# Around the turn from attention to MLP: squares summed earlier, three output-projection tiles ahead of the MLP's buffers, fewer small transfers, two loads issued from GpSimd

## The chip, the core and the metric

The kernel runs on one core of one Trainium2 chip. Its engines are TensorE (PE, matmuls; PEld is its weight load), VectorE (DVE), ScalarE (ACT), GpSimd (POOL) and SyncE (SP), which here does nothing but issue DMAs, in order. The metric is the device time of one execution in microseconds (us); lower is better.

## The reference

One step of a hybrid decoder layer in fp32: 512 prompt columns and 8 samples of 8 new columns (NT = 576 columns in all), model width D = 2048.

```python
h = x + W_out [ FoX(RMSNorm(x)) || DSA(RMSNorm(x)) ]
y = h + ConvGatedMLP(RMSNorm(h))
...
def rms_norm(x, g):
    y = xf * lax.rsqrt(jnp.mean(xf * xf, axis=-1, keepdims=True) + EPS)
    return y * g
...
def conv_ffn(hn, prev_g, w_gate, w_up, conv_w, conv_b, w_down):
    g = hn @ w_gate
    u = hn @ w_up
    gp = jnp.concatenate([prev_g, g], axis=1)
    gc = conv_b + sum(conv_w[j] * gp[:, j:j + T] for j in range(CONV_W))
    return (silu(gc) * u) @ w_down, gp[:, T:]
```

FoX is an attention with forget gates (8 heads), DSA a sparse attention over keys picked by an indexer (8 heads). The samples also attend to 1024 cached positions. The MLP's hidden width is 5504, which is 43 tiles of 128; its gate branch goes through a convolution of width 3 over positions, whose earlier rows come from the input `state_ffn_conv`, and whose last rows are outputs.

## The kernel before

Everything lies transposed in memory: 128 rows of the model dimension on the partitions, columns of the batch along the free axis. The 576 columns are cut in two halves of 288 (HALF): the first half is prompt alone, the second is the other 224 prompt columns and the 64 sample columns. A product of fp32 accuracy is made of three matmuls: each weight tile is cast to its upper part (ACT, `upper`, L1572 for the MLP's pools, tile `wu`), the rest is the lower part (DVE, `lower`, L1577, `wl`), and the matmuls are upper by upper, upper by lower and lower by upper (L1584, L1585, L1587).

Stages, in the order of the span: the input projection and the prompt's attention; the sample's DSA; the sample's FoX attention (`fox_scores`, `fox_values`), during which the output projection's other products fill TensorE (`w_out_a`, `w_out_late`, L171 to L173 with tile `rawT`, stored to the buffer `hdr` in DRAM); then the turn to the MLP; 43 items of gate and up projection; the down projection.

The turn is what the change rebuilds. It begins when the last sample's FoX result (`osum`) is turned and split into `gxs`. Three things follow in the code:

- The pools of the attention are closed and those of the MLP opened on the same memory. `wload` (L1566) brings a weight tile of 512 KB into one of four buffers `wr`.
- The loop over the 16 output tiles (`for o in range(KD)`): each tile's second half lacks the FoX heads' part, 8 products of 3 matmuls. The sum is added to `h` in DVE (L1667) and stored (L1668). `square` (L1592 to L1596) squares the tile's second half and two tiles of the first half on ACT and adds them up on DVE in `ssum`.
- `norm` makes the inverse root of the mean square from `ssum` by a matmul with ones (L1607) and Newton steps on DVE, and spreads it along the partitions as `rb`. `half0` normalizes the first half (16 multiplications `normed_h`, L1628) and splits it into `xh`, `xl` (L196 on ACT, L199 on DVE); it is a generator that the loop steps once per tile from the ninth tile on. `half1` does the same for the second half, interleaved with the first half's products (`products(0)` to `products(7)`), which are stored in the DRAM buffer `pdr`.

In the items, `states(j)` loads the convolution's earlier rows, eight DMAs of 16x128 for eight items (L1697); `last_rows(j)` collects seven items' last rows and stores them with fourteen DMAs (L1718, L1719). For the first eight items (`pre`), the products in `pdr` come back into `p1` and `gx` (L1907, L1908).

The order on each engine is not written out: a scheduler places the instructions of the whole program by its own estimate of times; where a tile's buffer is freed by an earlier user, the new user waits by semaphore. SP issues its DMAs strictly one after the other, so one that waits holds up all behind it.

## Time and profile before

| | us |
|---|---|
| median of three runs (2961.52, 2961.62, 2963.15) | 2961.62 |
| profiled execution | 2966.47 |
| its span | 2964.4 |
| PE busy in the span | 2773.7 (94%) |
| DVE busy | 2135.4 (72%) |
| ACT busy | 1414.1 (48%) |
| POOL busy | 501.6 (17%) |

Times in rows are counted from the start of the span. TensorE is the engine with the most work, and its busy time is close to the span, so what can be gained on it is idle time and time at the lower granted clock (PEclk, a share of full speed; about 0.5 is the lower level). In 700 us of the items, from 1650 to 2350, it is never idle. Matmuls are pipelined: the distance between two starts is what one costs, not the duration in its row. A bracket at a row's end is the engine's idle time before it and what ended that.

### The profile page before, as it was taken

The numbers are of one execution on the slowest core, as the hardware profiler recorded it, in microseconds if no ns is written. First come the engines' busy times: TensorE is split into PE (matmuls) and PEld (weight loads), VectorE is DVE, ScalarE is ACT, GpSimd is POOL, SyncE is SP. The second block draws the span as 40 slices with busy tenths as digits, with TensorE's granted clock in tenths as the row PEclk, the third lists the DMA queues.
The fourth block names the chain that finished last, engine by engine and source line by source line (L and its number), as shares of the span: only waits on it lengthen the run. The fifth ranks groups of instructions, "written<-read, shape, count | busy, mean of one in ns | idle before, by whom it ended". The sixth has DMA issues, their size and how long they took to land.

```text
span 2964.4 us, 52612 instructions
## 1 busy us (share of the span) xinstructions
PE 2773.7 (94%) x19863; PEld 2653.4 (90%) x19863; DVE 2135.4 (72%) x3732; ACT 1414.1 (48%) x2458; POOL 501.6 (17%) x579
## 2 busy tenths in 40 slices
PE   2999999999998999988989999999999989898998
PEld 2899899999898888868889999999999989888898
DVE  2667769656646656657977777777777789898996
ACT  2445753665755556654533444444444433333332
POOL 0223233423554133330000000000000000000000
PEclk7999999999999999989999999999999989999999
DMA  3523343335747788867544343343343353333333
GB/s 78 150 59 102 97 115 96 104 98 145 194 126 222 229 280 285 274 200 224 167 126 136 108 116 105 101 122 106 100 119 108 99 188 110 110 106 96 106 97 111
DMA packets 530956, 408.61 MB, mean 138 GB/s; under 512 B 41668, under 2 KB 472902, under 8 KB 530190
## 3 DMA queue, kind: packets, MB, share of 16 engines
q1 hardware_dynamic: 527294, 394.50, 45.4%
q0 software_dynamic: 3408, 10.75, 1.2%
q8 instruction: 156, 2.56, 0.4%
q14 instruction: 98, 0.80, 0.1%
HBM read 354.95 MB, written 49.95 MB: 137 GB/s over the span
## 4 chain that ended last, share of the span: by engine, by line
PE 50%; DVE 9%; DMA 7%; issue 2%; ACT 1%; SPq 1%; POOL 0%; DVEq 0%; ACTq 0%; POOLq 0%
PE pgemm L1584 8%; PE pgemm L1585 8%; PE pgemm L1587 7%; PE pone L1584 6%; PE pone L1585 5%; PE pone L1587 5%; DVE wl L1577 3%; DMA wr<-in_w_up_dram 2%; PE pone L1394 2%; DMA wr<-in_w_down_dram 1%; DVE ht L2084 1%; PE pgemm L171 1%; PE pgemm L172 1%; PE pgemm L173 1%; PE pout L1464 1%
## 5 line engine op out<-in xcount | busy, mean ns | idle before, releaser
L172 PE MATMUL pgemm<-xl,wh 128*128 128x288 f32 (+1 forms) x1696 | 512.2, 302 | 52.4 <-DVE xl L305 52.4
L171 PE MATMUL pgemm<-xh,wh 128*128 128x288 f32 (+1 forms) x1824 | 551.1, 304 | 4.7 <-DVE rawT L1340 2.1
L173 PE MATMUL pgemm<-xh,wl 128*128 128x288 f32 (+1 forms) x1824 | 550.4, 302 | 0.7 <-DVE wl L152 0.7
L172 PEld LDWEIGHTS pgemm<-xl,wh 128*128 128x128 f32 (+1 forms) x1696 | 322.3, 190 | 59.2 <-DVE xl L305 53.6
L171 PEld LDWEIGHTS pgemm<-xh,wh 128*128 128x128 f32 (+1 forms) x1824 | 346.0, 190 | 13.9 <-DVE rawT L1340 2.4
L1572 ACT CAST wu<-wr 128x1024 fp32r<-128x1024 f32 (+1 forms) x229 | 223.1, 978 | 275.0 <-PE pgemm L1585 109.3
L173 PEld LDWEIGHTS pgemm<-xh,wl 128*128 128x128 f32 (+1 forms) x1824 | 346.4, 190 | 6.6 <-issue 1.2
L1584 PE MATMUL pgemm<-xh,wu 128*128 128x288 f32 x1104 | 309.1, 303 | 39.4 <-DVE ht L2084 24.0
L1577 DVE TENSOR_TENSOR wl<-wr,wu 128x1024 fp32r<-128x1024 f32 (+1 forms) x229 | 258.3, 1133 | 120.9 <-ACT wu L1572 116.5
L1572 ACT CAST wu<-x 128x1024 fp32r<-128x1024 f32 x172 | 180.6, 1050 | 268.1 <-DVE x L1848 156.9
L1584 PEld LDWEIGHTS pgemm<-xh,wu 128*128 128x128 f32 x1104 | 212.8, 193 | 45.0 <-issue 20.4
L1584 PE MATMUL pgemm<-hi,wu 128*128 128x288 f32 x784 | 218.2, 303 | 5.4 <-DVE ht L2084 2.7
L1709 POOL COPY cn<-gx 128x2 f32<-128x2 f32 x43 | 45.8, 1065 | 1013.5 <-DVE gx L1725 1013.5
L1577 DVE TENSOR_TENSOR wl<-x,wu 128x1024 fp32r<-128x1024 f32 x172 | 209.1, 1219 | 1.6 <-ACT wu L1572 0.5
L1585 PE MATMUL pgemm<-lo,wu 128*128 128x288 f32 x760 | 209.9, 300 | 0.0
L1585 PE MATMUL pone<-xl,wu 128*128 128x288 f32 x768 | 208.9, 297 | 0.0
L1572 ACT CAST wu<-sum 128x768 fp32r<-128x768 f32 (+1 forms) x112 | 95.2, 850 | 234.7 <-DVE sum L1848 114.3
L1585 PE MATMUL pgemm<-xl,wu 128*128 128x288 f32 x680 | 185.8, 298 | 0.0
L1587 PE MATMUL pgemm<-xh,wl 128*128 128x288 f32 x1104 | 181.1, 297 | 0.0
L152 POOL TENSOR_TENSOR wl<-wraw,wh 128x1024 fp32r<-128x1024 f32 (+1 forms) x51 | 122.0, 2392 | 338.9 <-ACT wh L151 336.9
L151 ACT CAST wh<-wraw 128x1024 fp32r<-128x1024 f32 (+1 forms) x122 | 127.1, 1042 | 97.5 <-PE pgemm L172 89.9
L1584 PE MATMUL pone<-hi,wu 128*128 128x288 f32 x536 | 150.9, 304 | 19.9 <-ACT wu L1572 15.8
(616 smaller groups left out, 7377.1 us busy)
## 6 DMA issues: line engine op xcount, KB each, us to landing
wr<-in_w_gate_dram SPq DMA_DIRECT2D x102, 512.0 KB
wraw<-in_w_in_dram SPq DMA_DIRECT2D x88, 512.0 KB
wr<-in_w_up_dram SPq DMA_DIRECT2D x86, 512.0 KB
wr<-in_w_down_dram SPq DMA_DIRECT2D x112, 384.0 KB
kraw<-in_cache_fox_k_dram SPq DMA_DIRECT2D x128, 256.0 KB
vraw<-in_cache_fox_v_dram SPq DMA_DIRECT2D x128, 256.0 KB
wraw<-in_w_out_dram SPq DMA_DIRECT2D x32, 512.0 KB
dkraw<-in_cache_dsa_k_dram SPq DMA_DIRECT2D x64, 128.0 KB
```

The lines of the kernel that those rows point to most:

```text
L151: A.copy(h[:, :k, :m], raw[:, :k, :m])
L152: (G if share[0] and not u else V).tensor_sub(l[:, :k, :m], raw[:, :k, :m], f(h)[:, :k, :m])
L171: T.matmul(acc[:m, :], h[:, j, :m], xh[:, c], start=kt == 0, stop=False)
L172: T.matmul(acc[:m, :], h[:, j, :m], xl[:, c], start=False, stop=False)
L173: T.matmul(acc[:m, :], l[:, j, :m], xh[:, c], start=False, stop=kt == nk - 1)
L1394: T.transpose(pp[:, g * P:(g + 1) * P], raws[h // 4 * 4 + g][:, h % 4 * P:(h % 4 + 1) * P], ident)
L1572: A.copy(h[:, :n], t[:, :n])
L1577: V.tensor_sub(l[:, :n], t[:, :n], f(h)[:, :n])
L1584: T.matmul(acc, wh, xh, start=start and k == 0, stop=False, skip_group_check=not start)
L1585: T.matmul(acc, wh, xl, start=False, stop=False, skip_group_check=not start)
L1587: T.matmul(acc, wl, xh, start=False, stop=k == len(rows) - 1, skip_group_check=not start)
L1709: G.tensor_copy(c[:, j % CN, 0:2], gx[:, TP:TP + 2])
```

## The change

The first half's columns are complete in `w_out_a` and `w_out_late`, so their squares are taken there (`square0`), ACT and DVE each once per tile, and the inverse root `yn0` is made at the attention's end (`inverse_rms`), before the MLP's pools open. Three (NW) of the sixteen second-half tiles are computed at that place too, with weights that `load_w` has fetched into the attention's own buffers, and are stored to `hdr`; the loop in the MLP's pools then has thirteen tiles, and `half0` steps from the fifth tile on. Its sums alternate between two kinds of PSUM buffers. A group of eight loads of earlier rows becomes one DMA, a group of fourteen stores of last rows two. The loads from `pdr` are issued by GpSimd instead of SP.

```diff
+NW = 3
...
-    jobs += [([w_out[:1024, o * P:(o + 1) * P]], 8, P) for o in range(NLATE)]
+    jobs += [([w_out[:1024, o * P:(o + 1) * P]], 8, P) for o in (*range(NLATE), *range(NW))]
...
                 V.tensor_add(d, acc, d)
+                if o >= NLATE and not hh:
+                    square0(d)
...
             V.tensor_add(hx, acc, hx)
+            square0(hx)
...
+    def square0(d):
+        if not begun:
+            begun.append(1)
+            A.activation(ssum0, d, AF.Square)
+            return
+        sq = sx.tile([P, HALF], F32, name="sq0", bufs=2)
+        A.activation(sq, d, AF.Square)
+        V.tensor_add(ssum0, ssum0, sq)
...
+    yn0 = const.tile([P, 3], F32, name="yn0")
+    inverse_rms(sx, yn0, [ssum0])
+    for o in range(NW):
+        hx = wp.tile([P, NT], F32, name="rawT", bufs=3)[:, :HALF]
+        S.dma_start(hx, hdr[o, :, HALF:])
+        units = ready.pop(0)
+        prefetch(1)
+        gemm(units, gxs, P, lambda _, acc: V.tensor_add(hx, acc, hx), (1,))
+        S.dma_start(hdr[o, :, HALF:], hx)
     sx_ctx.close()
     sk_ctx.close()
...
     def half0():
-        yield from norm(ssum[0])
+        along(yn0)
+        yield
...
-    for o in range(KD):
-        load_wo(o + 4)
...
+    for o in range(NW, KD):
+        load_wo(o - NW + 4)
...
-        acc = psum_g()
+        acc = psum_g() if o % 2 else psum_s()[:, :HALF]
...
-        sq1 = square(o, 1)
-        if o < 8:
-            square(2 * o, 0)
-            square(2 * o + 1, 0)
-        else:
-            next(fox0, None)
+        if o - NW < NW:
+            square(o - NW)
+        sq1 = square(o)
         if o == 3:
             taps()
+        if o > 3:
+            next(fox0, None)
...
-            for i in range(m):
-                S.dma_start(st[i * 16:(i + 1) * 16, :], state[:, (j + i) * P:(j + i + 1) * P])
+            S.dma_start(st[:m * 16, :], state[:, j * P:(j + m) * P].rearrange("r (i c) -> i r c", c=P))
...
+            S.dma_start(cvp[:, jj].rearrange("r (i c) -> i r c", c=P), co[:m * 2, :])
+            S.dma_start(cvs[:, jj].rearrange("r (i c) -> i r c", c=P), co[m * 2:m * 18, :])
...
-            S.dma_start(p1, pdr[j, 0])
-            S.dma_start(gx[:, 2:2 + HALF], pdr[j, 1])
+            G.dma_start(p1, pdr[j, 0])
+            G.dma_start(gx[:, 2:2 + HALF], pdr[j, 1])
```

How the order moves at three places follows; line numbers of the changed kernel are one to some forty higher.

On SP, at the turn, before: after the convolution's taps (`gx`) come a load of `h` and at once the weights of the loop.

```order
L1554 DMA gx<-in_conv_w_dram 43x128 x3
L1555 DMA gx<-in_conv_b_dram 43x128
L1539 DMA x_17378<-hdr 128x4x288
L1566 DMA wr<-in_w_out_dram 128x8x128 x3
L1539 DMA x_17380<-hdr 128x8x288
L1539 DMA x_17379<-hdr 128x8x288
L1566 DMA wr<-in_w_out_dram 128x8x128
L1697 DMA stt<-in_state_ffn_conv_dram 16x128 x7
L1566 DMA wr<-in_w_out_dram 128x8x128
```

And in the changed kernel:

```order
L1596 DMA gx<-in_conv_w_dram 43x128 x3
L1597 DMA gx<-in_conv_b_dram 43x128
L1731 DMA stt<-in_state_ffn_conv_dram 128x1x128
L1551 DMA hdr<-rawT 128x288 x3
L1731 DMA stt<-in_state_ffn_conv_dram 128x1x128
L1608 DMA wr<-in_w_out_dram 128x8x128 x2
L1581 DMA x_17558<-hdr 128x2x288
L1608 DMA wr<-in_w_out_dram 128x8x128
L1581 DMA x_17558<-hdr 128x2x288
L1581 DMA x_17560<-hdr 128x8x288
```

The stores of the three tiles, each of which needs its tile's sum, now stand ahead of the first weight load of the loop, and so does the second load of earlier rows; the row of seven small loads is gone.

On DVE, at the end of the loop, before: the 16 multiplications of `half0`, the splits `xh` and `xl`, and then the first operation of the second half's norm (`ms`).

```order
L1596 TENSOR_TENSOR ssum_17390<-ssum_17390,sq 128x288
L1628 SCALAR_TENSOR_TENSOR x_17380<-x_17380,g_144,rb 128x288 x8
L1628 SCALAR_TENSOR_TENSOR x_17379<-x_17379,g_144,rb 128x288 x8
L1667 TENSOR_TENSOR x_17381<-pgemm,x_17381 128x288
L1577 TENSOR_TENSOR wl<-wr,wu 128x1024
L199 TENSOR_TENSOR xh<-x_17380,xh 128x8x288
L199 TENSOR_TENSOR xl<-x_17379,xl 128x8x288
L1611 TENSOR_SCALAR ms<-pone 128x2
```

In the changed kernel the same multiplications stand behind the third and fourth weight tile of the loop:

```order
L1619 TENSOR_TENSOR wl<-wr,wu 128x1024 x3
L1703 TENSOR_TENSOR x_17558<-pgemm,x_17558 128x288
L1703 TENSOR_TENSOR x_17558<-pone,x_17558 128x288
L1655 SCALAR_TENSOR_TENSOR x_17560<-x_17560,g_144,rb 128x288 x8
L1655 SCALAR_TENSOR_TENSOR x_17559<-x_17559,g_144,rb 128x288 x8
L1638 TENSOR_TENSOR ssum<-ssum,sq 128x288
L1703 TENSOR_TENSOR x_17558<-pgemm,x_17558 128x288
L1619 TENSOR_TENSOR wl<-wr,wu 128x1024
L200 TENSOR_TENSOR xh<-x_17560,xh 128x8x288
```

They have moved from the loop's end to its beginning, and with them the splits.

On PE, at the last sample of the attention, before: behind the transposes of the probabilities (L785, L790) come 31 filler matmuls of the output projection up to the first product with the values (`pout`), and 8 more behind the sixth; the last of these rows and what follows:

```order
L171 MATMUL pgemm<-xh,wh 128x288
L1464 MATMUL pout<-svh,ptile 64x512
L1465 MATMUL pout<-svl,ptile 64x512
L1464 MATMUL pout<-svh,ptile 64x512
L1465 MATMUL pout<-svl,ptile 64x512
L1464 MATMUL pout<-svh,ptile 64x512
L1465 MATMUL pout<-svl,ptile 64x512
L172 MATMUL pgemm<-xh,wh 128x288
```

In the changed kernel:

```order
L786 MATMUL pone<-ident,bt 128x64 x8
L791 MATMUL pone<-ident,bt 8x64
L173 MATMUL pgemm<-xh,wh 128x288
L174 MATMUL pgemm<-xh,wl 128x288
L172 MATMUL pgemm<-xh,wh 128x288
L173 MATMUL pgemm<-xh,wh 128x288
L174 MATMUL pgemm<-xh,wl 128x288
L172 MATMUL pgemm<-xh,wh 128x288
L173 MATMUL pgemm<-xh,wh 128x288
L174 MATMUL pgemm<-xh,wl 128x288
L1479 MATMUL pone<-ident,ob 128x64 x4
L1468 MATMUL pout<-svh,ptile 64x512
```

Eight filler matmuls stand there and none behind the sixth product; the other 31 are done before the transposes. Behind the last product come the sums of squares (L1510) and the 72 matmuls of the three tiles.

## Rows read from the trace of the kernel before

**Rows 1.** Stretches of the span: start and end us, length, then busy time of PE, PEld, DVE, ACT and POOL (number of instructions), the granted TensorE clock, the DMA engines' busy share and GB/s.

```profile
1280.00:1300.00 20.00, 20.00 (x124) 15.99 (x123) 9.90 (x19) 11.60 (x19) 8.64 (x6) 1.00 0.58 179
...
1320.00:1340.00 20.00, 13.33 (x85) 13.20 (x86) 7.75 (x15) 7.70 (x13) 0.00 (x0) 0.74 0.93 261
...
1360.00:1380.00 20.00, 19.37 (x146) 18.94 (x146) 16.63 (x40) 11.69 (x20) 0.00 (x0) 1.00 1.09 312
1380.00:1400.00 20.00, 13.26 (x78) 12.34 (x77) 19.34 (x43) 7.92 (x8) 0.00 (x0) 0.77 0.44 129
...
1460.00:1620.00 160.00, 142.03 (x1000) 139.92 (x999) 122.84 (x172) 59.82 (x66) 4.67 (x16) 0.95 0.47 136
1650.00:2350.00 700.00, 700.00 (x5276) 699.78 (x5275) 523.75 (x662) 321.97 (x417) 42.71 (x62) 1.00 0.38 108
```

**Rows 2.** The chain of waits from 1318 to 1330 us: start, us, what.

```profile
1320.65 5.59 DMA wr<-in_w_out_dram
1326.26 1.05 ACT wu L1572
```

**Rows 3.** PE instructions in time order, from the last sample's first `pout` to the fourth tile of the loop: start us, duration us, line, operation, output and inputs, shapes, count, and the idle time before with its releaser.

```profile
1303.39 0.40 PE L1464 MATMUL pout<-svh,ptile 128*64 128x512 f32 x1
...
1319.45 0.39 PE L1465 MATMUL pout<-vn,ptile 8*64 8x512 f32 x1
...
1327.36 0.61 PE L1584 MATMUL pgemm<-xh,wu 128*128 128x288 f32 x1 [6.16 <-ACT wu L1572]
...
1328.96 0.44 PE L1584 MATMUL pgemm<-xh,wu 128*128 128x288 f32 x1
1329.20 0.44 PE L1585 MATMUL pgemm<-xl,wu 128*128 128x288 f32 x1
...
1338.29 1.22 PE L1587 MATMUL pgemm<-xh,wl 128*128 128x288 f32 x8
...
1345.07 0.29 PE L1585 MATMUL pgemm<-xl,wu 128*128 128x288 f32 x1
1345.20 0.29 PE L1584 MATMUL pgemm<-xh,wu 128*128 128x288 f32 x1
```

**Rows 4.** PE in time order at the end of the loop; the columns are those of group 3.

```profile
1385.63 0.82 PE L1587 MATMUL pgemm<-xh,wl 128*128 128x288 f32 x5
...
1390.74 0.61 PE L1584 MATMUL pgemm<-xh,wu 128*128 128x288 f32 x1 [4.18 <-ACT xh L196]
...
1396.19 0.61 PE L1585 MATMUL pgemm<-xh,wu 128*128 128x288 f32 x1
```

**Rows 5.** DVE in time order: the split of the last attention result into `xl`, and the end of the loop.

```profile
1322.13 0.69 DVE L199 TENSOR_TENSOR xl<-osum,xh 128x512 fp32r<-128x512 f32 x1 [0.68 <-ACT xh L196]
...
1385.02 6.96 DVE L1628 SCALAR_TENSOR_TENSOR x<-x,g,rb 128x288 f32<-128x288 f32 x16 [0.32 <-ACT rb L1623]
1391.89 0.45 DVE L1667 TENSOR_TENSOR x<-pgemm,x 128x288 f32<-128x288 f32 x1
...
1393.39 2.55 DVE L199 TENSOR_TENSOR xh<-x,xh 128x2304 fp32r<-128x2304 f32 x1
...
1398.33 0.16 DVE L1611 TENSOR_SCALAR ms<-pone 128x2 f32<-128x2 f32 x1
```

**Rows 6.** The tile `ssum` over the whole span: line, engine, operation, count, duration in ns (least, median, most), first and last start.

```profile
L1596 DVE TENSOR_TENSOR ssum<-ssum,sq x29: 437/452/461, 1334.0 to 1384.3; 128x288 f32<-128x288 f32 x29
...
L1594 ACT ACTIVATE ssum<-x x2: 429/437/445, 1333.2 to 1333.8; 128x288 f32<-128x288 f32 x2
```

**Rows 7.** SP's issues in time order, at the beginning of the loop.

```profile
1327.95 2.00 SPq L1566 DMA_DIRECT2D wr<-in_w_out_dram  x1
1330.00 6.80 SPq L1697 DMA_DIRECT2D stt<-in_state_ffn_conv_dram  x7
1338.23 0.39 SPq L1566 DMA_DIRECT2D wr<-in_w_out_dram  x1
```

**Rows 8.** SP's issues in time order, in the items from 1561 to 1604 us.

```profile
1561.48 0.37 SPq L1566 DMA_DIRECT2D wr<-in_w_up_dram  x1
...
1581.07 0.37 SPq L1566 DMA_DIRECT2D wr<-in_w_up_dram  x1
...
1597.45 5.80 SPq L1697 DMA_DIRECT2D stt<-in_state_ffn_conv_dram  x6
1603.35 0.39 SPq L1566 DMA_DIRECT2D wr<-in_w_up_dram  x1
```

**Rows 9.** Who waited for whom from 1440 to 1625 us, for SP and PE: us in total, times, longest.

```profile
SPq L1908 <- DVE x L1735: 36.7, 6, 9.1
SPq L1566 <- DVE x L1853: 36.0, 8, 8.9
...
PE pone L1584 <- ACT wu L1572: 15.8, 7, 3.7
```

**Rows 10.** DVE, POOL and SP at the last sample of the attention: in time order the `ptile` split and the last splits of the cached values, and among SP's waits from 1290 to 1450 us the one for a store.

```profile
1299.78 0.69 DVE L788 TENSOR_TENSOR ptile<-pone,ptile 128x512 fp32r<-128x512 f32 x1 [4.49 <-ACT ptile L787]
...
1313.50 4.19 POOL L199 TENSOR_TENSOR svl<-vraw,svh 128x512 fp32r<-128x512 f32 x3 [1.29 <-ACT svh L196]
...
SPq L1355 <- DMA hdr<-rawT: 3.7, 1, 3.7
```

**Rows 11.** The tile `dvraw`, whose loads are DMAs issued by GpSimd: duration in ns of an issue (least, median, most), first and last start.

```profile
L253 POOL DMA_INDIRECT dvraw<-in_cache_dsa_v_dram,pt x32: 946/964/1652, 700.5 to 877.1; - x32
```

More of the change, by code (lines that the diff above doesn't have):

```diff
@@ L1483, in fox_values, with inverse_rms @@
         yield
+    HB3 = [(t, min(P, HALF - t * P)) for t in range(3)]
+    onec = const.tile([P, 1], F32, name="onec")
+    V.memset(onec, 1.0)
+    ssum0 = sx.tile([P, HALF], F32, name="ssum0")
+    begun = []
+    def square0(d):
[6 more added lines that the diff above has]
+        V.tensor_add(ssum0, ssum0, sq)
+    def inverse_rms(pool, out, sums):
+        acc = psum_s()
+        for t, n in HB3:
+            for k, part in enumerate(sums):
+                T.matmul(acc[:n, t:t + 1], part[:, t * P:t * P + n], onec, start=k == 0, stop=k == len(sums) - 1)
+        ms = pool.tile([P, 3], F32, name="ms")
+        V.memset(ms, 1.0)
+        V.tensor_scalar(ms[:, 0:2], acc[:, 0:2], 1.0 / D, EPS, op0=OP.mult, op1=OP.add)
+        V.tensor_scalar(ms[:32, 2:3], acc[:32, 2:3], 1.0 / D, EPS, op0=OP.mult, op1=OP.add)
+        yn = newton(pool, ms, [P, 3], "n4")
+        V.tensor_scalar(out, yn, -0.125, None, op0=OP.mult)
     lane("sa", 2.068)
@@ L1548, in tile_hymba_step @@
     cw = fn.tile([P, 4, NF], F32, name="cw")
-    ssum = [wb.tile([P, HALF], F32, name=f"ssum{i}") for i in range(2)]
+    ssum = wb.tile([P, HALF], F32, name="ssum")
     ones = wb.tile([P, P], F32, name="ones")
@@ L1590, in rows8, with square, along @@
         return [(w[0][:, k * P:(k + 1) * P], w[1][:, k * P:(k + 1) * P], x[0][:, k, :], x[1][:, k, :]) for k in range(8)]
-    def square(o, half):
-        sq = wb.tile([P, HALF], F32, name="sq", bufs=2) if o else ssum[half]
-        A.activation(sq, hh(o, half), AF.Square)
-        if 0 < o and not (half and o == KD - 1):
-            V.tensor_add(ssum[half], ssum[half], sq)
+    def square(o):
+        sq = wb.tile([P, HALF], F32, name="sq", bufs=2) if o else ssum
+        A.activation(sq, hh(o, 1), AF.Square)
+        if 0 < o < KD - 1:
+            V.tensor_add(ssum, ssum, sq)
         return sq
     rb = [None]
-    def norm(*sums):
+    def along(yn):
         acc = psum_s()
-        blocks = [(t, min(P, HALF - t * P)) for t in range(3)]
-        for t, n in blocks:
-            for k, part in enumerate(sums):
-                T.matmul(acc[:n, t:t + 1], part[:, t * P:t * P + n], ones[:, 0:1], start=k == 0,
-                         stop=k == len(sums) - 1)
-        ms = wb.tile([P, 3], F32, name="ms")
-        V.memset(ms, 1.0)
-        V.tensor_scalar(ms[:, 0:2], acc[:, 0:2], 1.0 / D, EPS, op0=OP.mult, op1=OP.add)
-        V.tensor_scalar(ms[:32, 2:3], acc[:32, 2:3], 1.0 / D, EPS, op0=OP.mult, op1=OP.add)
-        yn = newton(wb, ms, [P, 3], "n4")
-        V.tensor_scalar(yn, yn, -0.125, None, op0=OP.mult)
-        yield
-        acc = psum_s()
-        for t, n in blocks:
+        for t, n in HB3:
             dg = wb.tile([P, P], F32, name="dg", bufs=3)
@@ L1623, in norm @@
         A.copy(rb[0], acc[:, :HALF])
-        yield
     def normed_h(o, half):
@@ L1782, in half1 @@
     def half1():
-        yield from norm(ssum[1], sq1)
+        yn = wb.tile([P, 3], F32, name="yn")
+        inverse_rms(wb, yn, [ssum, sq1])
+        yield
+        along(yn)
+        yield
         for o in range(8):
```

39 lines of the change are left out of this document (22 added, 17 removed).

## The prediction

> **What bounds the kernel now.** I first read the stretches [rows 1]. From 1650 to 2350 us PE is busy 700 of 700 us at full clock: nothing that the change does to other engines can show there. What it can win lies where PE has idle time: at the turn (13.33 of 20 us busy at clock 0.74, later 13.26 of 20 at 0.77) and in the first items (142.03 of 160). Around 1280 PE is busy 20.00 of 20 while DVE has 9.90 and ACT 11.60: there it pays for nothing that ACT and DVE take on, as long as they stay below it.
>
> Then the chain and the time order. The attention's last `pout` starts at 1319.45 [rows 3]. The loop's first weights are issued at 1320.65, land after 5.59 us, are cast in 1.05 us [rows 2], and PE starts at 1327.36 after 6.16 us idle [rows 3]. Starts are then 0.24 us apart (1328.96, 1329.20), later 0.13 (1345.07, 1345.20) [rows 3]. That is the first gap. The loop ends at 1386.45 (1385.63 + 0.82) [rows 4]. The second gap follows: DVE is in the 16 multiplications from 1385.02 for 6.96 us, adds the last tile at 1391.89, and makes two splits of 2.55 us from 1393.39, before `ms`, the start of the second half's norm, at 1398.33 [rows 5]. PE restarts at 1390.74 for a matmul and again at 1396.19 [rows 4]. So 1398.33 - 1386.45 = 11.9 us lie between the last product and that norm.
>
> In the first items I looked at SP [rows 8]. The weights of the up projection are issued at 1561.48 and 1581.07, a period of 19.6 us; the next should be at 1600.7, but six small loads take SP 5.80 us from 1597.45, and it comes at 1603.35, 2.7 us late.
>
> **The change, part by part.** I sum against the profiled execution, 2966.47 us, which is 4.85 above the median of the runs, and subtract that at the end.
>
> *Squares beside the attention.* Added there: 16 on ACT of 0.437 us = 7.0 us, 15 sums on DVE of 0.452 = 6.8 us [rows 6], spread over w_out tiles under a PE that is full [rows 1]. Cover: the filler matmuls. Where it is thin (the last sample), they delay casts that `pout` needs. Bounds 0 and 3 us lost; I take 1.0.
>
> *The attention's tail.* The order puts 31 filler matmuls ahead of the last transposes that were behind them: at 0.133 us [rows 3], the transposes come 4.1 us later. `ptile` was ready at 1300.47 (1299.78 + 0.69) [rows 10], 2.9 us before the first `pout` at 1303.39 [rows 3] used it. So 1.2 us are left. SP gets new loads of `h` tiles behind stores; one such wait took 3.7 us [rows 10]. I add 1.1, about a third of one, since `pout` ended on the last splits of values (POOL to 1317.69, 1313.50 + 4.19 [rows 10], last `pout` 1319.45 [rows 3]), so a load that comes late shows only in part. Sum: 2.3 us later; bounds 0 and 6.
>
> *The three tiles.* The split `xl` of the attention's result ended at 1322.82 (1322.13 + 0.69) [rows 5], so they can start at 1325.1. They are 72 matmuls. After the first gap the slow pace lasted from 1327.36 for some 5.3 us, 22 matmuls at 0.24; I charge the same: 22 x 0.24 + 50 x 0.133 = 11.9 us, end 1337.0. The loop's first load stands on SP behind the stores of these tiles and a load whose buffer a PE transpose behind the tiles frees. The add of the last tile (0.46, as at 1391.89 [rows 5]) and one to two issues on SP make 1.5 us: issue at 1338.5. It landed in 5.59 us before [rows 2], behind a load of `h` of 0.59 MB, which at 312 GB/s [rows 1] is 1.9 us; so 3.7 to 5.6, and I take 4.3, nearer the low end since that load of `h` now comes after two weights. With the cast, 1.1, the first of the 13 tiles starts at 1343.9. The fourth tile of before began at 1339.5 (1338.29 + 1.22) [rows 3]. So the first gap isn't removed: it moves behind the three tiles, and PE is cold after it once more.
>
> *Thirteen tiles.* Before, they took 1339.5 to 1386.45 = 46.9 us, of which 13 x 24 x 0.133 = 41.5 are matmuls and 5.4 waits. After: 41.5, a cold start of 22 x 0.107 = 2.4, and 3 for weights. Not more than before, because the seven small loads of 6.80 us, which held the fifth weight load to 1338.23 [rows 7], are one; not much less, because DVE now has the 6.96 and 5.1 us of multiplications and splits [rows 5] inside the loop, where it was busy 16.63 of 20 us [rows 1], less the first half's 15 sums of 0.45. Sum 46.9: end 1390.8; bounds 1388, without the 3 for weights, and 1397, if half of the 12.1 us moved on DVE shows.
>
> *The second gap.* The norm waits then for the last add, square and sums of ones only: 0.45 + 0.44 [rows 5, 6] and about 1.4 for the ones and semaphores: 1390.8 + 2.3 = 1393.1 against 1398.33. That gains 5.2 us; by the bounds 8.0 (1398.3 - 1388 - 2.3) to -1.0. What is late next is DVE itself, whose work on the second half follows directly, so I let the gain through whole.
>
> *Few small DMAs.* In the items the 2.7 us of [rows 8] go, because PE there waits for casts of the weights (15.8 us in 7 waits [rows 9]). Bounds 0 and 4. The later groups lie under PE's full stretch [rows 1]: nothing. One DMA of 128 rows instead of eight of 16 moves the same bytes.
>
> *GpSimd issues.* `gx` waits on SP for its buffer, 36.7 us in six waits; but the weight load behind it waits for its own buffer too (36.0 in eight) [rows 9]. Freeing SP buys nothing: 0. Cost: 16 issues of 0.964 us [rows 11] on POOL, busy 4.67 of 160 us there [rows 1], 15.4 us hidden by that idleness, if the waits on POOL don't hold up its copies of last rows. Bounds 1 gained, 11.8 lost (rival D). The Trainium skill ("DMA: Bandwidth & Descriptors", Issuing engines are not separate DMA queues) says that the issuing engine changes only the sequencer's time to issue, since all run on the same 16 DMA engines. By that, too, the sum gets 0.
>
> Sum: 1.0 - 5.2 - 2.7 = -6.9 (the tail's 2.3 is inside the 5.2): 2966.47 - 6.9 = 2959.6 profiled, less 4.85: 2954.7 us.
>
> **Rivals.**
>
> A. The loop's weights come earlier: if their buffers lie on memory that frees before the three tiles end, loads start beside them, and the idle stretch (1337.0 to 1343.9) and the second cold start go: 6.9 + 2.4 = 9.3 less 1.5 for other waits, 7.8 more: 2946.9. For: 11.9 us of matmuls cover a load of 5.59. Against: the order on SP.
>
> B. The turn gives nothing: DVE, with 12.1 us of moved work in the loop, ends it at 1396 (1390.8 + 5.2), and only the 2.7 less 1.0 stay: 2961.62 - 1.7 = 2959.9. For: 19.34 of 20 in DVE's stretch [rows 1]. Against: the multiplications moved to the loop's start, where DVE waits for weights.
>
> C. Slower: in the last sample, loads of `h` stand on SP ahead of value loads, and each waits for its store to land, 3.7 us [rows 10]; the filler that covered PE is gone from there. Four whole waits, 14.8 + 1.2 = 16.0 in place of 2.3, turn -6.9 into +6.8: 2968.4. It decides from the third whole wait on (11.1 + 1.2: +3.1). For: the filler's place. Against: one such wait in the rows.
>
> D. The issues on GpSimd hold up DVE, or come late, in the eight items: if each of 16 issues stopped DVE for its 0.964 us [rows 11], 15.4 us, of which DVE's idle share, 37 of 160 us [rows 1], takes 3.6, up to 11.8 would show; I price half, since PE is ahead of DVE at times: 2954.7 + 5.9 = 2960.6. The Trainium skill ("SBUF — State Buffer", the trap "DVE blocks DMA") speaks against this part of the change: GpSimd writes descriptors through ports shared with DVE under an exclusive lock. No row here has a GpSimd issue beside such DVE work; by it the time would be D's.
>
> **How the numbers follow.** Forecast 0.45, with a range of its own of 2950 to 2960 by the bounds above; A 0.15, B 0.18, C 0.13, D 0.09. A measurement of this kernel can't tell less than 0.2%, 5.9 us: faster is below 2955.7, slower above 2967.5. Three quarters of the forecast and all of A, with a little of B and D, are faster: 0.52. C but for its mild forms, and a little of D: 0.13. The rest, 0.35, is the same. The range, 2945 to 2965, takes in A, B, D and the forecast's bounds, and leaves out C's far part and the best end of A.
>
> **What would show it.** Right: PE idle some 6 us twice around 1321 to 1344, the first product of the loop at about 1344, its end near 1391, `ms` within 3 us of the last add, no SP row of several `stt`, the up projection's load at 19.6 us after the one before. A shows as `wr` loads issued before 1337; B as DVE without idle time and `ms` after 1396; C as the last `pout` after 1325; D as longer waits of PE for `wu` than 15.8 us. Wrong outright: gains or losses before 1280 or after 1650.

## The result: 0.6% slower

| | us |
|---|---|
| before, median of five runs | 2961.52 (2958.23 to 2963.15) |
| after, median of five runs | 2976.55 (2973.07 to 2982.41) |
| ratio, over all runs | 1.0063, 95% interval 1.0051 to 1.0075 (the two medians alone give 1.0051) |
| predicted | 2954.7 (2945 to 2965), slower with a chance of 0.13 |
| profiled execution after, and its span | 2976.55, 2974.8 |

The two traces are compared by four stretches that every kernel here has: the *turn* (end of the attention's last `pout` to the first sum of a gate row, `gx`), the *first items* (to the ninth gate row), the *other items* (to the last gate row), and the *down projection* (to the end).

| us | turn | first items | other items | down projection |
|---|---|---|---|---|
| before | 144.6 | 159.5 | 758.4 | 582.1 |
| after | 144.8 | 159.9 | 759.9 | 590.9 |

The spans differ by 10.4 us, and 8.8 of it lie in the down projection, which the prediction never priced. (These are single executions; equal code differed by up to 6 us in that stretch, as the experiments show.) For the turn, with the attention's tail and the squares counted in, the sum had a gain of 4.2; it gave nothing. Neither did the first items, which were to gain 2.7.

The stretches of the changed kernel, with the columns of [rows 1]; the first, the third and the last two are stretches of [rows 1].

```profile
1320.00:1340.00 20.00, 14.76 (x87) 13.55 (x87) 5.85 (x30) 1.19 (x3) 0.00 (x0) 0.78 0.18 54
1340.00:1360.00 20.00, 15.96 (x91) 15.57 (x92) 11.90 (x23) 7.88 (x10) 0.00 (x0) 0.76 1.13 327
1380.00:1400.00 20.00, 20.00 (x157) 19.97 (x156) 13.71 (x30) 10.35 (x16) 0.00 (x0) 1.00 1.02 281
1440.00:1460.00 20.00, 15.89 (x99) 15.43 (x98) 17.07 (x16) 7.71 (x11) 0.54 (x1) 0.83 0.42 124
...
1460.00:1620.00 160.00, 141.62 (x990) 139.78 (x989) 121.87 (x172) 57.99 (x64) 9.59 (x29) 0.94 0.49 136
1650.00:2350.00 700.00, 700.00 (x5272) 699.78 (x5271) 522.16 (x660) 321.77 (x416) 42.66 (x62) 1.00 0.38 108
```

The same view of the kernel before, for one stretch more:

```profile
1440.00:1460.00 20.00, 18.73 (x140) 18.27 (x139) 16.45 (x15) 8.02 (x11) 0.00 (x0) 1.00 0.65 183
```

Between 1380 and 1400 PE is now busy 20.00 of 20 us where it had 13.26: the second gap is gone there. Sixty microseconds later it has 15.89 where it had 18.73: the lead is lost again. Look also at the DMA columns: while the three tiles run, the DMA engines move 54 GB/s, where before they moved 261.

PE of the changed kernel in time order, with the columns of [rows 3]:

```profile
1318.90 0.39 PE L1469 MATMUL pout<-vn,ptile 8*64 8x512 f32 x1
...
1321.58 0.85 PE L172 MATMUL pgemm<-xh,wh 128*128 128x288 f32 x2 [0.41 <-ACT xh L197]
...
1341.89 0.61 PE L1626 MATMUL pgemm<-xh,wu 128*128 128x288 f32 x1 [6.08 <-ACT wu L1614]
...
1396.40 0.28 PE L1510 MATMUL pone<-onec,ssum 128*128 128x1 f32 x2
1396.54 0.91 PE L1629 MATMUL pgemm<-xh,wl 128*128 128x288 f32 x5
...
1398.03 0.20 PE L1510 MATMUL pone<-onec,sq 128*32 128x1 f32 x2
```

SP of the changed kernel in time order, at the turn and in the items:

```profile
1315.44 0.93 SPq L1731 DMA_DIRECT2D stt<-in_state_ffn_conv_dram  x1
1328.73 6.89 SPq L1551 DMA_DIRECT2D hdr<-rawT  x3
1335.84 0.65 SPq L1731 DMA_DIRECT2D stt<-in_state_ffn_conv_dram  x1
1336.54 1.08 SPq L1608 DMA_DIRECT2D wr<-in_w_out_dram  x2
...
1582.24 0.37 SPq L1608 DMA_DIRECT2D wr<-in_w_up_dram  x1
...
1601.63 0.37 SPq L1608 DMA_DIRECT2D wr<-in_w_up_dram  x1
```

DVE of the changed kernel in time order, from the add of the last tile to the first multiplication of the second half, and ACT beside it:

```profile
1391.23 0.45 DVE L1703 TENSOR_TENSOR x<-pgemm,x 128x288 f32<-128x288 f32 x1
...
1398.27 0.16 DVE L1513 TENSOR_SCALAR ms<-pone 128x2 f32<-128x2 f32 x1 [2.65 <-PE pone L1510]
...
1401.70 1.23 DVE L1619 TENSOR_TENSOR wl<-wr,wu 128x1024 fp32r<-128x1024 f32 x1 [0.83 <-ACT wu L1614]
...
1402.91 1.22 DVE L1619 TENSOR_TENSOR wl<-wr,wu 128x1024 fp32r<-128x1024 f32 x1
...
1408.95 1.38 DVE L1655 SCALAR_TENSOR_TENSOR x<-x,g,rb 128x288 f32<-128x288 f32 x3 [3.89 <-ACT rb L1651]
```

```profile
1393.28 1.05 ACT L1614 CAST wu<-wr 128x1024 fp32r<-128x1024 f32 x1 [1.45 <-PE pgemm L1627]
1394.23 0.44 ACT L1636 ACTIVATE sq<-x 128x288 f32<-128x288 f32 x1
```

The last tile's add is done at 1391.68, but its square starts at 1394.23, behind a weight cast; the matmuls with ones that take it end at 1398.23, behind products. The same place before, ACT at the last square, PE at the matmuls with ones, and DVE at the first multiplication of the second half:

```profile
1394.03 0.44 ACT L1594 ACTIVATE sq<-x 128x288 f32<-128x288 f32 x1
```

```profile
1394.52 0.59 PE L1607 MATMUL pone<-ones,sq 128*128 128x1 f32 x2 [1.51 <-ACT sq L1594]
...
1396.02 0.24 PE L1607 MATMUL pone<-ones,sq 128*32 128x1 f32 x2
```

```profile
1409.09 6.96 DVE L1628 SCALAR_TENSOR_TENSOR x<-x,g,rb 128x288 f32<-128x288 f32 x16
```

There PE stood idle for the square and took it at once, and the matmuls with ones ended at 1396.26; the two splits on DVE held `ms` to 1398.33 [rows 5].

In the down projection, DVE's waits for the loads of its weights (us in total, times, longest), 480 us from the last gate row on; first before, then after:

```profile
DVE sum L1848 <- DMA wr<-in_w_down_dram: 10.8, 16, 1.7
```

```profile
DVE sum L1885 <- DMA wr<-in_w_down_dram: 22.2, 17, 2.7
```

These two rows differ by 11.4 us, more than the 8.8 that the stretch lost, for the same 112 loads of 384 KB in both kernels. These waits show on PE, which waits there for `ht`, written by DVE; from the last gate row to the end, before and after:

```profile
PE pgemm L1584 <- DVE ht L2084: 34.4, 21, 4.2
```

```profile
PE pgemm L1626 <- DVE ht L2121: 41.4, 29, 4.2
```

In the chain of work that ended last, loads of these weights are 7.5% of the stretch before and 10.0% after. The DMA engines are no fuller: busy share 0.36 before, 0.35 after, over the 480 us.

### The profile page after: what moved, and what is told of

Its sections match the earlier page's. It is cut to its first block, busy times and chain, and to the rows that moved or that the text cites. A ratio compares the mean times of both kernels' runs of the same rounds, so it can differ in the third digit from the quotient of the medians.

```text
span 2974.8 us, 52512 instructions
## 1 busy us (share of the span) xinstructions
PE 2777.7 (93%) x19863; PEld 2654.6 (89%) x19863; DVE 2140.8 (72%) x3733; ACT 1413.1 (48%) x2458; POOL 508.9 (17%) x595
## 4 chain that ended last, share of the span: by engine, by line
PE 51%; DVE 8%; DMA 7%; issue 1%; ACT 1%; SPq 0%; POOL 0%; DVEq 0%; ACTq 0%
PE pgemm L1626 8%; PE pgemm L1627 8%; PE pgemm L1629 8%; PE pone L1626 6%; PE pone L1627 6%; PE pone L1629 5%; DVE wl L1619 3%; DMA wr<-in_w_down_dram 2%; PE pgemm L173 1%; PE pone L1398 1%; PE pgemm L174 1%; PE pgemm L172 1%; DVE ht L2121 1%; DMA wr<-in_w_up_dram 1%; DMA vraw<-in_cache_fox_v_dram 1%
## 5 line engine op out<-in xcount | busy, mean ns | idle before, releaser
L173 PE MATMUL pgemm<-xl,wh 128*128 128x288 f32 (+1 forms) x1720 | 518.6, 302 | 54.5 <-DVE xl L306 54.2
L172 PE MATMUL pgemm<-xh,wh 128*128 128x288 f32 (+1 forms) x1848 | 557.7, 303 | 3.4 <-ACT wh L152 1.7
L174 PE MATMUL pgemm<-xh,wl 128*128 128x288 f32 (+1 forms) x1848 | 556.9, 302 | 0.7 <-DVE wl L153 0.7
L1626 PE MATMUL pgemm<-xh,wu 128*128 128x288 f32 x1032 | 288.8, 302 | 30.7 <-DVE ht L2121 22.8
L1626 PEld LDWEIGHTS pgemm<-xh,wu 128*128 128x128 f32 x1032 | 198.2, 192 | 37.4 <-issue 19.5
L1627 PE MATMUL pone<-xl,wu 128*128 128x288 f32 x816 | 222.4, 298 | 0.0
L1629 PE MATMUL pgemm<-xh,wl 128*128 128x288 f32 x1032 | 171.0, 298 | 0.0
L1627 PE MATMUL pgemm<-xl,wu 128*128 128x288 f32 x608 | 166.9, 299 | 0.0
```

Of the source, the lines that this page charges most:

```text
L172: T.matmul(acc[:m, :], h[:, j, :m], xh[:, c], start=kt == 0, stop=False)
L173: T.matmul(acc[:m, :], h[:, j, :m], xl[:, c], start=False, stop=False)
L174: T.matmul(acc[:m, :], l[:, j, :m], xh[:, c], start=False, stop=kt == nk - 1)
L1626: T.matmul(acc, wh, xh, start=start and k == 0, stop=False, skip_group_check=not start)
L1627: T.matmul(acc, wh, xl, start=False, stop=False, skip_group_check=not start)
L1629: T.matmul(acc, wl, xh, start=False, stop=k == len(rows) - 1, skip_group_check=not start)
```

## The experiments

All kernels compute the whole output. The times by stretch come from one profiled execution each; two executions of equal code (before and `b_same`, `a_psumg` and `a_psumg2`) differed by up to 6 us in the down projection and up to 4 at the turn, so the ratios decide. Each comes from 5 to 12 runs of a kernel and, in the experiments, from 18 to 29 of the kernel before on the same chip. The last column is DVE's wait for down-projection weights, as in the two rows above.

| kernel | turn | first items | down | ratio to before, 95% | wait |
|---|---|---|---|---|---|
| b_same | 144.0 | 158.5 | 577.4 | 1.0011 [1.0001, 1.0021] | 10.6 |
| b_gps | 144.2 | 160.5 | 579.8 | 1.0008 [0.9998, 1.0018] | 12.9 |
| b_few | 142.0 | 156.1 | 581.7 | 0.9992 [0.9981, 1.0003] | 15.8 |
| b_pad | 144.3 | 158.3 | 579.3 | 1.0011 [1.0000, 1.0022] | 10.9 |
| b_loads | 140.0 | 155.7 | 581.9 | 0.9985 [0.9971, 0.9998] | 16.4 |
| b_alt | 154.0 | 159.7 | 585.5 | 1.0044 [1.0029, 1.0059] | 16.8 |
| after | 144.8 | 159.9 | 590.9 | 1.0063 [1.0051, 1.0075] | 22.2 |
| a_sp | 144.3 | 158.9 | 589.6 | 1.0068 [1.0055, 1.0081] | 21.9 |
| a_nw0 | 133.4 | 159.4 | 592.0 | 1.0016 [1.0005, 1.0027] | 22.4 |
| a_nw4 | 141.6 | 161.6 | 593.3 | 1.0049 [1.0034, 1.0064] | 21.8 |
| a_psumg | 146.3 | 158.6 | 594.9 | 1.0058 [1.0046, 1.0070] | 26.6 |
| a_psumg2 | 142.5 | 159.5 | 588.9 | 1.0053 [1.0036, 1.0070] | 22.3 |
| a_store_act | 144.3 | 160.3 | 584.8 | 1.0044 [1.0029, 1.0059] | 19.0 |
| a_pad3 | 144.6 | 157.4 | 588.0 | 1.0039 [1.0026, 1.0052] | 18.3 |
| a_psumg_pad6 | 141.8 | 159.5 | 592.2 | 1.0059 [1.0039, 1.0079] | 20.6 |
| sq_pg | 132.8 | 157.5 | 578.7 | 0.9956 [0.9943, 0.9969] | 13.8 |
| sq_few_pg | 132.5 | 159.5 | 583.5 | 0.9994 [0.9982, 1.0007] | 17.8 |
| sq_w3 | 142.3 | 158.7 | 585.1 | 1.0015 [1.0004, 1.0026] | 15.8 |
| a_many | 143.7 | 161.4 | 585.6 | 1.0023 [1.0011, 1.0035] | 17.2 |

The waits go with the length of the down projection: 10.6 to 16.4 us with 577 to 582, 15.8 to 19.0 with 583 to 588, over 20 with 589 to 595. So does the share that loads of these weights have in the chain of work that ended last: 5.4 to 7.9% of the stretch with 577 to 582, 8.0 to 12.0% with 588 to 595.

### The small parts by themselves

`b_same` is the kernel before, unchanged: a control, which shows that differences of 0.1% are not to be read. The others put one part into the kernel before (b_) or take it out of the changed one (a_).

```diff
# b_gps (before); a_sp is the reverse, in the changed kernel
-            S.dma_start(p1, pdr[j, 0])
+            G.dma_start(p1, pdr[j, 0])
# b_few (before): eight loads in one, fourteen stores in two
-                S.dma_start(st[i * 16:(i + 1) * 16, :], ...)
+            S.dma_start(st[:m * 16, :], ...)
```

Expected of `b_same`: 

> The kernel before, unchanged, as a control. In the two traces so far the down projection, whose instructions stand in the same order on every engine, takes from the 4000th matmul before the end 604 us before and 613 after the change. Theory P (the change made the down projection slower for good, through something that it moved, such as a buffer's place or the weight loads' phase): this kernel takes 2961.5 (2958 to 2964) and its down projection again 604 to 606 us. Rival R (one execution differs from the next by that much, whatever the kernel): its down projection takes anything between 604 and 613, and times scatter by 10 us.

Of `b_gps`: 

> The kernel before, with the 16 loads of p1 and gx issued by GpSimd, and nothing else changed. Theory P with the turn as the place of the first part: same as before within 3 us, since no weight load waited for these loads. Rival G (issues on GpSimd hold up DVE or come late): 2966 to 2974, with the loss in the first eight items (1450 to 1610 us).

Of `b_few`: 

> The kernel before, with one load of eight items' earlier rows and two stores of seven items' last rows, and nothing else changed. By what I forecast (2.7 us, the late load of up weights at 1603) it is 2958 to 2960. Theory now: the load is earlier by those 2.7 us, yet PE is full from 1600 on, so the time is the same, 2960 to 2963. Rival F (large transfers of these rows come in the way of weight loads, in the down projection's time too): 2966 or more.

Of `a_sp`: 

> The changed kernel, with p1 and gx issued by SP again. Theory P without GpSimd: 2973 to 2979, as the changed kernel. Rival G: 2961 to 2968.

GpSimd's issues do nothing: `b_gps` lies at the control, `a_sp` at the changed kernel. The few transfers alone take about 0.2% less than the control (the intervals just overlap), with first items of 156.1 instead of 158.5 us. That may be the 2.7 us of the prediction, but the runs don't show it: `b_loads`, below, keeps the many transfers and has 155.7. One sentence of the expectations was wrong: the order of the down projection is *not* the same in all kernels. The scheduler orders the whole program, and an edit at the turn changes the order 1000 us later.

### Tiles, addresses and PSUM buffers

```diff
# a_nw0, a_nw4 (changed kernel); a_nw4, with NW = 4, also has the taps and half0's steps one tile later
-NW = 3
+NW = 0
# b_pad (before): two small tiles more, later buffers 64 bytes further on
+    onec = const.tile([P, 1], F32, name="onec")
+    yn0 = const.tile([P, 3], F32, name="yn0")
# a_psumg (changed kernel; a_psumg2 is the same again); b_alt is the reverse, in before
-        acc = psum_g() if o % 2 else psum_s()[:, :HALF]
+        acc = psum_g()
```

Of `a_nw0`: 

> The changed kernel with NW = 0: the first half's squares stay beside the attention, all sixteen second-half tiles stay in the MLP's buffers. Measured so far, in us from the last item's gate row to the end: before 577 to 582, changed 590 and 591; this loss of 10 is not from the few transfers and not from GpSimd. Theory T (the three tiles cause it, by the count of weight tiles that go through the rotating buffers, 13 instead of 16): 577 to 582 again, the kernel at 2958 to 2964. Rival S (the squares' two constant tiles, which lie ahead of all later buffers and move them by 64 bytes): 588 to 592, the kernel at 2970 to 2978.

Of `a_nw4`: 

> The changed kernel with NW = 4, so that twelve weight tiles go through the four rotating buffers, a whole number of turns as with sixteen, and what follows stands in the same buffers as before the change. Theory T: the down projection is back at 577 to 582 us, the kernel at 2962 to 2968. Rivals S and U: 588 to 592, 2972 to 2978. Either way the turn itself, from the attention's last product to the first gate row, stays at 144 to 145 us if the second half's norm sets its length.

Of `b_pad`: 

> The kernel before with the two constant tiles of the change (onec, yn0) made and set to one, and used by nothing: they only move the later buffers in SBUF by 64 bytes. Rival S: the down projection takes 588 to 592 us from the last item's gate row, and the kernel 2968 to 2972. Theory T: 577 to 582, 2958 to 2963.

Of `a_psumg`: 

> The changed kernel with the loop's thirteen sums all in the pool of two PSUM buffers, as before the change, and no longer in turn with the pool of four. Third theory U (the turn of the PSUM buffers, shifted by the seven sums taken from the other pool, makes the down projection wait): 577 to 582 us from the last gate row, the kernel at 2962 to 2968. Theories T and S: 589 to 592, 2972 to 2978.

Of `b_alt`: 

> The kernel before with one line of the change: the sixteen sums of the loop go in turn to the pool of two and the pool of four PSUM buffers. In its down projection (from the last gate row on) the instructions stand, on PE, ACT, DVE and SP, in exactly the order of a_psumg, which has the rest of the change and not this line; I had earlier taken the down projection's order to be the same in all kernels, and it is not. Theory O (the loss of 10 to 15 us there comes with the order that the scheduler makes of the down projection, whatever edit moved it): 592 to 597 us there, 144 at the turn, the kernel at 2972 to 2978. Rival (squares or tiles cost it there): 577 to 582, the kernel at 2958 to 2964.

Without the three tiles the turn is 11.4 us shorter (133.4), so the squares, with the weight loads that now come first, do gain there and the tiles give it all back; a fourth tile takes no more. The addresses do nothing (1.0011, as the control). For the down projection theories T, S and U all fell: it took 592.0 us without the tiles, 579.3 with the addresses alone moved and 594.9 with one kind of PSUM buffer. For the alternating PSUM buffers the runs speak against a single effect: in the kernel before they cost 10 us at the turn, and little in the down projection (585.5 us in exactly the order of `a_psumg`, where theory O gave 592 to 597), and in the changed kernel taking them out gains nothing that can be told.

### Weights first, stores elsewhere, squares alone

```diff
# b_loads (before): two weight loads ahead of the loads of h
-    load_h(0, 4, 1)
...
+    load_wo(2)
+    load_h(0, 2, 1)
     load_wo(3)
+    load_h(2, 4, 1)
# a_store_act (changed kernel): the three tiles' stores
-        S.dma_start(hdr[o, :, HALF:], hx)
+        A.dma_start(hdr[o, :, HALF:], hx)
# sq_pg (changed kernel): NW = 0, many small transfers, issues on SP, psum_g() alone
```

Of `b_loads`: 

> The kernel before with the loop's first two weight loads ahead of the loads of h, in the order of the changed source, and nothing else. In a_nw0 the weights were issued at 1316, before the attention's end, and the first gap was 1.4 instead of 6.2 us. Theory L (this order alone takes the first gap, and the squares only the second): the turn takes 138 to 141 instead of 144. Rival (the early issue needs the squares' edit): 144 again. The down projection has an order of its own: 577 to 597.

Of `a_store_act`: 

> The changed kernel with the three tiles' stores issued by ACT instead of SP, so that the loop's first weight loads stand on SP ahead of nothing but the second load of earlier rows. Theory W (the turn gains nothing with three tiles because SP holds the weight loads behind the tiles' stores): the turn takes 133 to 139 us instead of 144.8, PE's idle time before the loop falls from 6.1 to under 3. Rival (the second load of earlier rows, which waits for a PE transpose behind the tiles, holds them as well): 143 to 146 and 5 to 6 idle. Its down projection has an order of its own, so theory O gives no number there: 577 to 597.

Of `sq_pg`: 

> The changed kernel with NW = 0, with small transfers and issues as before the change and all sums in the pool of two: the squares beside the attention alone (with the order of loads that came with them). Its down projection has exactly the order of b_few (582 us). Theory O: 580 to 583 there, 131 to 137 at the turn as in a_nw0 (133), the kernel at 2948 to 2953: faster than before by 0.3%. Rival: 590 to 592, the kernel at 2958 to 2964.

`b_loads`, PE in time order at the loop's first product:

```profile
1317.96 0.61 PE L1584 MATMUL pgemm<-xh,wu 128*128 128x288 f32 x1 [1.94 <-ACT wu L1572]
```

The 6.16 us of the first gap [rows 3] became 1.94, and the turn 140.0 us. So the gap was a matter of SP's order alone, and no tiles are needed against it. `a_store_act`, SP in time order:

```profile
1314.73 21.12 SPq L1731 DMA_DIRECT2D stt<-in_state_ffn_conv_dram  x2
1335.89 1.09 SPq L1608 DMA_DIRECT2D wr<-in_w_out_dram  x2
```

With the stores gone from SP, the second load of earlier rows holds it instead, until a PE transpose behind the tiles frees its buffer; the first weights come at 1335.89, as late as in the changed kernel (1336.54), and the turn is 144.3 us: the rival held. No run has the tiles with neither their stores nor that load ahead of the weights, so what the tiles would cost then is not shown.

`sq_pg` is the best version found, 0.44% faster than before by the ratio over all runs (0.30% by the medians, 2949.18 us against 2958.09). Its DVE in time order, from the add of the last tile to the second half's norm:

```profile
1388.89 0.46 DVE L1705 TENSOR_TENSOR x<-pgemm,x 128x288 f32<-128x288 f32 x1 [1.20 <-PE pgemm L1631]
...
1393.48 0.15 DVE L1513 TENSOR_SCALAR ms<-pone 128x2 f32<-128x2 f32 x1
...
1396.50 0.17 DVE L1516 TENSOR_SCALAR yn<-n_y 128x3 f32<-128x3 f32 x1
...
1400.86 1.37 DVE L1657 SCALAR_TENSOR_TENSOR x<-x,g,rb 128x288 f32<-128x288 f32 x3
```

From `ms` to the first multiplication it takes 7.4 us. In the changed kernel that was 10.7: two weight splits of 1.2 us stand among the Newton steps, and `rb` comes later. In the kernel before it was as long, 10.8 (1398.33 to 1409.09).

### Is it the order of the down projection?

The memsets below write an unused tile; they move the scheduler's estimates, and with them the order of the down projection on each engine, to that of `b_few` (`a_pad3`) and nearly that of `b_loads` (`a_psumg_pad6`).

```diff
+    pad = yb.tile([P, 1024], F32, name="pad")
+    V.memset(pad, 0.0)
...
# sq_few_pg: sq_pg with the few transfers
```

Of `a_pad3`: 

> The changed kernel, whole, with three memsets of a tile that nothing uses (128x1024, DVE) ahead of the down projection. They shift the scheduler's own clock, and with it the down projection gets the order that it has in b_few and sq_pg (the same on SP, PE and DVE, four places apart on ACT), where it took 582 and 579 us. Theory O (the loss there comes with the order): 579 to 585 us from the last gate row, 144 at the turn, the kernel at 2962 to 2967, some 10 less than the changed kernel although it does more. Rival V (something else in the change, such as where buffers lie or what was in flight before, slows it): 590 to 594 and 2974 to 2980.

Of `a_psumg_pad6`: 

> a_psumg with six such memsets: the down projection then has the order of b_loads (the same on SP and DVE, 4 and 9 places apart on ACT and PE), where it took 582 us. Theory O: 580 to 586 against the 595 of a_psumg, the kernel at 2963 to 2969. Rival V: 592 to 597, 2975 to 2981.

Of `a_psumg2`: 

> a_psumg once more, unchanged. b_alt has the same order in the down projection and took 585.5 us there, a_psumg 594.9. If executions scatter by that much, this one may take anything from 584 to 596; if not, 593 to 597, and the order alone doesn't set the loss.

Of `sq_few_pg`: 

> sq_pg with the few small transfers on top (squares beside the attention, all sixteen tiles in the MLP's buffers, issues on SP). The turn at 133 as in sq_pg; the first eight items 155 to 156 as in b_few, where the eight loads of earlier rows are one. Its down projection has an order that no run has had: 578 to 595. With 580 the kernel is at 2945 to 2949, 3 under sq_pg; with 592 at 2958 to 2962.

The orders of kernels with 582 us gave 588.0 and 592.2 us here, so the order by itself isn't the cause; in `a_pad3` it may be some of it (1.0039 against 1.0063 of the changed kernel). `a_psumg2` against `a_psumg` is the scatter: 588.9 and 594.9 us of the same code. And `sq_few_pg` loses what `sq_pg` won: beside the squares the few transfers cost 0.38%.

### Squares and tiles; all but the few transfers

`sq_w3` is `sq_pg` with NW = 3. `a_many` is the changed kernel with the many small transfers of before.

Of `sq_w3`: 

> The version with the squares alone, with the three tiles put in and nothing else: issues on SP, the small transfers of before, one kind of PSUM buffer. Theory W (the three tiles cost at the turn what the squares gained, by the stores and the load of earlier rows that stand ahead of the first weight load): turn 144 us instead of 132.8. For the down projection theory F (it takes the few transfers and a new order together): 577 to 583 us and 2961 in all, ratio 0.999 to 1.002. Theory T (the tiles lengthen it too): 588 to 595 us, ratio 1.004 to 1.007. If the turn stays below 137, theory W is wrong.

Of `a_many`: 

> The changed kernel with the many small transfers of before in place of the few; all else as changed. Theory F (the few transfers take part in the loss of the down projection): last gate row to end 577 to 584 us instead of 590.9, first items 1 to 3 us longer than the 159.9 of the changed kernel, and a ratio of 1.000 to 1.002. Theory T (the loss comes with the three tiles): 588 to 595 us, ratio 1.005 to 1.007.

Both theories named one culprit for the down projection, and both fell: each kernel has about 585 us, between the two ranges. By their ratios, 1.0015 and 1.0023, the two lie nearer to theory F, and the first items of `a_many` are 1.5 us longer than the changed kernel's, as F forecast. For the turn theory W holds (142.3 us; its 144 was a little high). The rows of `sq_pg`, from the attention's end to `ms` with the first 24 us of it, and then those of `sq_w3`, are the ones to compare; the columns are those of [rows 1].

```profile
1324.00:1393.50 69.50, 60.73 (x446) 59.19 (x446) 52.41 (x97) 34.39 (x45) 0.00 (x0) 0.95 0.95 269
1324.00:1348.00 24.00, 19.10 (x133) 18.33 (x132) 20.29 (x53) 12.21 (x15) 0.00 (x0) 0.86 0.98 275
```

```profile
1316.00:1395.10 79.10, 65.15 (x445) 62.98 (x445) 49.23 (x93) 31.67 (x42) 0.00 (x0) 0.89 0.81 230
1316.00:1340.00 24.00, 15.73 (x98) 14.54 (x98) 6.95 (x31) 3.54 (x7) 0.00 (x0) 0.79 0.30 85
```

SP of `sq_w3` in time order:

```profile
1331.27 0.34 SPq L1551 DMA_DIRECT2D hdr<-rawT  x1
1332.33 1.24 SPq L1734 DMA_DIRECT2D stt<-in_state_ffn_conv_dram  x3
1333.61 1.05 SPq L1610 DMA_DIRECT2D wr<-in_w_out_dram  x2
```

PE runs the same matmuls (445 and 446 in the rows) in 9.6 us more. In the first 24 us the DMA engines move 85 GB/s instead of 275: SP issues the first weights of the loop at 1333.61, behind the last of the tiles' stores and loads of earlier rows, and the loads of `h` after them.

The runs give a path from before to after, one or two edits at a time, in per cent of the time before (each step uncertain by about 0.17, from two intervals of 0.12; the steps add up to the whole by construction):

| step | kernels | per cent |
|---|---|---|
| squares beside the attention, weights ahead of `h` | before to sq_pg | -0.44 |
| three tiles | sq_pg to sq_w3 | +0.59 |
| PSUM buffers in turn, GpSimd's issues | sq_w3 to a_many | +0.08 |
| few transfers | a_many to after | +0.40 |
| sum | | +0.63 |

The steps that were also made elsewhere agree: tiles +0.47 (`a_nw0` to after), few transfers +0.38 (`sq_pg` to `sq_few_pg`). Taken from the medians, the four steps are -0.30, +0.47, +0.08 and +0.26: the same signs, but smaller. Only in the kernel before do the few transfers cost nothing.

## Why the prediction was wrong

*The squares and the attention's tail.* Forecast 1.0 us lost and 2.3 us later. The last `pout` ended at 1319.3 against 1319.8, but this end lay between 1312.7 and 1324.6 in the kernels here, and at 1323.2 in `b_same`, so neither term can be told from nothing. Rival C is out: no end after 1325 belongs to the changed kernel.

*The three tiles.* The mechanism was right, and the time within 2 us: the gap moved behind them, 6.08 us, and the loop's first product stands at 1341.89 where 1343.9 was forecast. The slow pace of the tiles was seen, too. Rival A is out: the first weights were issued at 1336.54, behind the stores. (That is before the 1337 that A named as its sign, but the tiles were done by then: their last matmul ended at 1334.77.) Up to the loop's end the forecast stands. What the step left out shows only against a turn without the tiles: what stood still meanwhile. It priced the tiles on PE and their weights, and not the loads held back: 54 GB/s instead of 261 [rows 1] in 20 us is 4.1 MB that come later, of which the tiles' own weights, 3 x 0.52 MB, were there already; the 2.6 MB left take 8 us at the 327 GB/s of the next stretch. That estimate is close to the 9.5 us that the tiles cost at the turn (132.8 to 142.3); that the loads held back are the whole of it is argued, since no run holds them back alone.

*Thirteen tiles.* End forecast at 1390.8. The add of the last tile starts at 1391.23, so the end was right; but the loop had begun 2 us earlier than forecast, so it took some 2 us more than the 46.9, and the two misses cancel.

*The second gap.* This is the step that failed: "The norm waits then for the last add, square and sums of ones only". `ms` came at 1398.27, against 1398.33 [rows 5], in place of 1393.1, and 7.0 us after the start of the last add where 2.3 were forecast. The term of about 1.4 us for ones and semaphores left out what stands in front of the norm's steps on ACT and PE. The first half's products now followed without a gap, and theirs stood in front: on ACT a weight cast that waited for PE held the last square for 2.55 us (1391.68 to 1394.23); on PE the matmuls with ones, done in idle time before, stood between products and ended at 1398.23, 3.6 us after the square's end (1394.67). Behind `ms` nothing was gained either: the first multiplication came at 1408.95, against 1409.09 before. PE, by count of matmuls started, was 42 ahead at 1400 (8977 against 8935), and 2 ahead at 1460 (9350 against 9348): it had waited for that chain. In `sq_pg` `ms` follows 4.6 us after the start of the last add and in the changed kernel 7.0, so part of the loss is the new order. From the attention's end to `ms` the forecast amounts to 71.0 us, 78.5 before (1319.84 to 1398.33 [rows 3, 5]) less 5.2 and 2.3; the changed kernel takes 79.0 and `sq_pg` 69.5. So the gain that the sum had was there to be had, without the three tiles, which the sum had at some 2 us (1343.9 against 1339.5, less the tail's 2.3) and which took 9.5. Not all of it is the squares': in `sq_pg` the weights also come first, and `b_loads`, with that alone, has a turn 4.6 us shorter than before. Rival B had the outcome (the turn gives nothing, `ms` after 1396) by another cause: DVE was not full, 13.71 of 20 us.

*Few transfers.* The period of the up projection's loads did go from 22.3 [rows 8] to 19.4 us (1582.24 to 1601.63), as forecast, but the first items stayed at 159.9, with PE's waits for the casts `wu`, which the term was to shorten, at 21.6 us instead of 15.8 [rows 9]. With the many transfers the first items of the changed kernel take 161.4 (`a_many`), so some 1.5 us may be gained and lost again in the rest of the change. "The later groups lie under PE's full stretch [rows 1]: nothing" failed: with the squares the few transfers cost 0.4% of the whole time.

*GpSimd issues.* Forecast 0, found 0. An issue took 0.54 us instead of 0.964 [rows 11], and DVE's busy time in the items is about the same (121.87 against 122.84 us [rows 1]). Rival D is out: `b_gps` at 1.0008 stands beside a control of 1.0011. Its sign, PE's waits for `wu` above 15.8 us, did appear (21.6), but with the issues back on SP they are 21.1 (`a_sp`). The trap of the Trainium skill ("SBUF — State Buffer", the trap "DVE blocks DMA") is stated for DVE operations in a two-port mode, such as an fp32 copy from SBUF to SBUF. From 1404 to 1592 us, where the 16 issues stand, the changed kernel's DVE has seven such copies, 1.2 us in all, so these runs hardly test it.

*The down projection.* The largest error isn't in a term of the sum; it is a stretch that had none. From 700 of 700 us busy until 2350 the prediction went straight to the end, and named anything after 1650 only as "wrong outright". The last 582 us have waits of their own, and DVE's 10.8 us for weights were in the trace of before. It was a stretch put at nothing without a reason, and it measured 8.8 us. The runs don't show one edit that lengthens it. The steps that tiles (578.7 to 585.1) and few transfers (585.6 to 590.9; 578.7 to 583.5) make in single traces are 5 to 6 us, as much as equal code differs, and without the tiles the changed kernel still takes 592.0 (`a_nw0`). What holds over all kernels is this: those with the many transfers or without the squares stay at 577 to 586, and all of 588 to 595 have the squares and the few transfers together with at least one more part of the change. `a_store_act`, at 584.8, has them too. GpSimd's issues, the addresses and the order don't do it alone. By the ratios the few transfers beside the squares cost some 11 us of 2960, which neither the turn nor the first items show, so part of it probably lies here; that is argued, not shown. The traces show where the time goes: DVE waits for weights. Why the same loads are waited for longer stays open.

## What to carry to other kernels

Work that is moved ahead of a turn must not put a store, or a load whose buffer is still in use, on the issuing queue ahead of the next stage's loads: here the turn waited for the first weights and `h`, and putting two weight loads in front (`b_loads`) did without cost what three early tiles failed to do. Where a scheduler orders the whole program, read the waits of every stage that isn't full, however far from the edit, and leave room in the range for it. Build the parts one by one: the bundle lost 0.63%, and the squares with the weight loads in front gained 0.44%.

## What the runs showed that was not expected

- Filling PE's idle time didn't bring the chain of small steps forward: `ms` at 1398.3 with PE busy 13.26 of 20 us, and at the same time with 20.00. Before, the matmuls with ones ended 1.8 us after the last square (1394.47 to 1396.26); between products, 3.6 us.
- Gains don't add up: few transfers -0.2% against the control in the kernel before, +0.4% beside the squares.
- DVE's waits for 112 equal loads ranged from 10.6 (`b_same`) to 26.6 us (`a_psumg`), with no edit in that stage in either.
- Alternating two kinds of PSUM buffers in the 16-tile loop cost 10 us at the turn in the kernel before (`b_alt`, 0.33% against the control), and nothing that can be told in the changed kernel. The runs don't say why.
